# An encoder layer in f32 on one core: x is turned as it comes and kept feature-major, and the row lengths are applied in the splits

## The chip, the cores and the metric

The kernel runs on one core of one Trainium2 chip. The core has TensorE (PE, matrix products; PEld loads its weights), VectorE (DVE), ScalarE (ACT), GpSimd (POOL) and SyncE (SP), whose queue issues nearly all DMAs of this kernel; sixteen DMA engines move the data between the large memory (DRAM) and the core's own memory (SBUF). Products go to a small accumulator memory (PSUM), of which a tile of two banks holds the sums of a whole output tile. The metric is the device time in microseconds. The figure for a kernel is the median of its runs; beside it stands one profiled execution, to which all durations of the profile belong.

## The reference

One layer of a hybrid encoder is computed for a prompt of 512 rows and a sample of 64 rows, with 2048 features. What matters here is its beginning and the first residual sum:

```python
mod = jax.nn.silu(c) @ w_ada[l] + b_ada[l]
sh1, sc1, g1, sh2, sc2, g2 = jnp.split(mod[:, None, :], N_MOD, axis=-1)
h = rmsnorm(x, norm1[l]) * (1 + sc1) + sh1
mix, s_a, s_b, s_c = token_mixers(h, ...)     # h @ w_in, GLA, gated DeltaNet, @ w_out
x = x + g1 * mix
h = rmsnorm(x, norm2[l]) * (1 + sc2) + sh2    # then the FFN, the second residual sum, the final norm
```

`rmsnorm` divides each row of x by the root of its mean square (plus 1e-6). The prompt and the sample have their own modulation (`c_prompt`, `c_sample`). So x is needed twice: normed and modulated, as the input of the projections, and untouched, as the first term of the residual sum.

## The kernel before

All activations are held feature-major: 128 features on the partitions, the 576 rows (512 of the prompt, 64 of the sample) along a tile as two halves of 288, each 256 prompt rows and 32 sample rows (`HP` = 256, `HT` = 288). There are `KD` = 16 such tiles. A product in f32 precision is made of three in the faster form `fp32r`: each operand is split into a high and a low part (ACT copies the rounded high part, DVE subtracts it), and high x high, low x high and high x low are summed in PSUM (`mm6`, lines 544 and 546). Every weight tile of 512 KB passes this way: a DMA into a raw tile, `split` (lines 630 to 632) into `wh` and `wl`, products.

**The head** (`head`, from line 641) computes the modulation, brings x in, and makes the input tiles `h`. `modulation(g)` multiplies the conditioning vectors with a block of w_ada: for each of two parts (scale and shift) it goes through 16 row blocks, two at a time, in 8 steps; each step loads 512 KB into an `hraw` tile (a ring of five). Steps at rows 4 and 12 multiply the raw tile as it is in whole f32 (line 710), the others split it and multiply the parts (lines 714 and 715). The sums are turned by small products (line 720). The first call, `modulation(0)`, has 16 steps, and ahead of steps 1, 3, 5, 7 and 9 (`X_AT`) it brings in one block of x: `x_block(b)` loads 128 rows (64 for the sample) in four pieces of 512 features, sums their squares on ACT (line 673), makes the reciprocal root on DVE and POOL (lines 674, 140, 141), scales the four pieces on DVE (line 677), and turns them on PE (line 682) into PSUM, from where ACT copies them into `xT` (lines 685 and 689). Then, for g = 0 to 3, `modulation(g + 1)` is followed by the four input tiles of group g: `split_mod` makes s * xT + b on DVE (line 566), the high part on ACT (567) and the low part on DVE (568), and the tile goes at once into the narrow gates (line 829) and the first q and k projections.

**The mixers** follow, in which PE runs the projections (`in_tile`) and between them, at each tick, a step of the recurrences or of the rest of the modulation (`ada`, line 772, with tiles `xr` and `ax`).

**The residual stage** then forms w_out times the second half of the mixers' output: for each of 16 feature tiles m, 8 blocks of products (48 of them), and beside them x: `x_load(m)` reads the 128 columns of tile m from the row-major input into an `xr` tile (a ring of two, which the last modulation tiles and the loads of the mixers' output `od` also use), and `x_tile(m)` turns it by five transpositions on PE (line 147, called by `transpose4`, and line 1129) and copies it on ACT into the place of an old `h` tile (lines 1127 and 1130). `residual` adds the gated product on DVE (line 1096). The first half of the mixers' output follows in a second pass over the same tiles, then the FFN.

The order of instructions on each engine, SP's DMAs among them, is fixed when the program is built: the framework's scheduler takes them by the order in which the code emits them, as far as its own cost model has their inputs and places ready. A block under `high_priority(offset=80)` is ranked 80 instructions earlier; all weight loads and splits are. `pgt` gives PSUM tiles from a ring of two.

Of the kernel before, what the change touches and what calls it, by code (L numbers as in the profile page):

```python
# [27 lines left out]
X_AT = (1, 3, 5, 7, 9)  # L28
# [70 lines left out]
class Kern:  # L99
# [462 lines left out]
    def split_mod(self, x, s, b, hh, hl, tmp):  # L562

        nc = self.nc
        for c, q in ((slice(0, HP), 0), (slice(HP, HT), 1)):
            nc.vector.tensor_scalar(tmp[:, :, c], x[:, :, c], s[:, q:q + 1], b[:, q:q + 1], op0=ALU.mult, op1=ALU.add)
        nc.scalar.activation(hh, tmp, AF.Copy)
        nc.vector.tensor_tensor(hl, tmp, hh.bitcast(F32), op=ALU.subtract)
# [70 lines left out]
    def head(self, pool):  # L639
# [25 lines left out]
        def x_block(b):  # L665
            n = P if b < 4 else TS
            xt = [slot() for _ in range(4)]
            for q in range(4):
                f = slice(q * 512, (q + 1) * 512)
                nc.sync.dma_start(xt[q][:n], i["x_prompt"][0, b * P:(b + 1) * P, f] if b < 4 else i["x_sample"][0, :, f])  # L670
            ms4 = pool.tile([P, 8], F32, tag="ms4", bufs=2, name=self.name("ms4"))
            for q in range(4):
                A.activation(junk[:n], xt[q][:n], AF.Square, scale=float(D) ** -0.5, accum_out=ms4[:n, q:q + 1])
            V.tensor_reduce(ms4[:n, 4:5], ms4[:n, 0:4], axis=mybir.AxisListType.X, op=ALU.add)
            self.rsqrt(ms4[:, 5:6], ms4[:, 4:5], 1, n)
            for q in range(4):
                V.tensor_scalar_mul(xt[q][:n], xt[q][:n], ms4[:n, 5:6])
            per = 4 if b < 4 else 8
            for k0 in range(0, KD, per):
                ps = self.pgt()[:, 0]  # L680
                for k in range(k0, k0 + per):
                    T.transpose(ps[:, (k - k0) * n:(k - k0 + 1) * n], xt[k // 4][:n, k % 4 * P:(k % 4 + 1) * P],
                                self.c["ident"][:n, :n])
# [7 lines left out]


# [4 lines left out]
        hraw = lambda: pool.tile([P, 1024], F32, tag="hraw", bufs=5, name=self.name("hraw"))  # L697
# [415 lines left out]
    def x_load(self, m):  # L1113

        nc, i, raw = self.nc, self.i, self.xr()
        n = slice(m * P, (m + 1) * P)
        nc.sync.dma_start(raw[:, :512].rearrange("p (b t) -> p b t", b=4), i["x_prompt"][0, :, n].rearrange("(b p) n -> p b n", p=P))
        nc.sync.dma_start(raw[:TS, 512:512 + P], i["x_sample"][0, :, n])
        return raw

    def x_tile(self, m, raw):

        nc = self.nc
        t = self.slot(self.x_place(m), F32)
        nc.gpsimd.memset(t[:, :, HP:ZS], 0.0)
        ps = self.transpose4(raw[:, :512].rearrange("p (b t) -> p b t", b=4))
        nc.scalar.activation(t[:, :, :HP], ps.rearrange("p (h b) t -> p h (b t)", h=2), AF.Copy)
        ps = self.bank()
        nc.tensor.transpose(ps[:, :TS], raw[:TS, 512:512 + P], self.c["ident"][:TS, :TS])
        nc.scalar.activation(t[:, :, ZS:], self.halves(ps[:, :TS]), AF.Copy)  # L1130
        return t

# [431 lines left out]
def layer_kernel(tc, i, o):  # L1564
    nc = tc.nc
    with ExitStack() as ctx:
# [10 lines left out]
        nc.vector.memset(K.zero3, 0.0)  # L1577
        K.xd = [dp.tile([P, 2, HZ], F32, name=f"xd{m}") for m in range(KD)]
# [3 lines left out]
        with ExitStack() as early:  # L1582
            K.wp = pool(early, "wp", "right", bufs=3)
            with ExitStack() as right:
# [9 lines left out]
                with ExitStack() as st:  # L1594
# [126 lines left out]
```

## Time and profile before

| | |
|---|---|
| median of 3 runs | 2973.34 us (2972.37 to 2979.27) |
| the profiled execution | 2975.75 us, span 2974.0 us |
| mean granted clock of TensorE | 0.989 of full |
| PE busy | 2892.8 us, 97% of the span |
| DVE, ACT, POOL busy | 2106.4, 1232.6, 359.1 us |
| moved by DMA | 393.02 MB, mean 132 GB/s |

A row of the profile names the line of the kernel, the engine, the operation, and the tiles written and read (out<-in, buffer numbers left out), with a count. Busy time is the time in which an engine executes; the idle time is put down to whatever released the engine. The chain of waits goes back from the last instruction, at each step to what it waited for. The granted clock is the share of full clock that TensorE was given. Matmul ends are modelled, so the starts of successive instructions are the safer measure of PE's pace. "Whole f32" products show two records each.

### The profile page before, as it was taken

How to read it: one execution, taken by the hardware profiler on the slowest of the kernel's cores; microseconds unless marked ns; L12 is line 12 of the kernel's file. 1: busy time of each engine (PE TensorE's matmuls, PEld its weight loads, DVE VectorE, ACT ScalarE, POOL GpSimd, SP SyncE). 2: the span in 40 equal slices, each digit the busy share in tenths (PEclk: the TensorE clock that was granted, in tenths of full speed). 3: DMA queues.
4: the chain of work that ended last, by engine and by line, in shares of the span. 5: the costliest groups of instructions: out<-in, count | busy, mean ns of one | idle time of the engine just before them, and what ended most of it. 6: DMA issues, size and time to landing. Idle time of an engine off the chain costs nothing.

```text
span 2974.0 us, 52340 instructions
## 1 busy us (share of the span) xinstructions
PE 2892.8 (97%) x21128; PEld 2786.1 (94%) x21128; DVE 2106.4 (71%) x3243; ACT 1232.6 (41%) x2124; POOL 359.1 (12%) x616
## 2 busy tenths in 40 slices
PE   7998999998999999999999999999999999999998
PEld 3588999998989998999999999999999999999997
DVE  5786777775669777367888888888888865555555
ACT  6573544544244433255444444444444422222223
POOL 0015433343310001000000000000000000000000
PEclk8999999999999999999999999999999999999999
DMA  7864455544545447443333333333333463333221
GB/s 263 283 176 142 141 158 151 153 138 129 148 129 149 142 136 210 134 130 90 101 111 98 105 109 109 100 104 109 104 106 98 140 230 98 114 102 112 85 84 66
DMA packets 509446, 393.02 MB, mean 132 GB/s; under 512 B 41385, under 2 KB 438404, under 8 KB 509204
## 3 DMA queue, kind: packets, MB, share of 16 engines
q1 hardware_dynamic: 503780, 379.00, 42.8%
q0 software_dynamic: 5424, 10.68, 1.2%
q8 instruction: 167, 2.74, 0.4%
q14 instruction: 75, 0.61, 0.1%
HBM read 355.23 MB, written 34.36 MB: 131 GB/s over the span
## 4 chain that ended last, share of the span: by engine, by line
PE 86%; DVE 4%; POOL 3%; DMA 2%; issue 2%; ACT 2%; ACTq 0%; SPq 0%; POOLq 0%; DVEq 0%
PE g L544 29%; PE g L546 14%; PE g L1330 8%; PE g L1331 8%; PE g L1332 8%; PE bank L1331 3%; PE bank L1330 3%; PE bank L1332 3%; PE bank L147 1%; DVE acc L772 1%; PE bank L778 1%; POOL m L359 1%; PE bank L419 1%; POOL m L360 1%; PE bank L710 1%
## 5 line engine op out<-in xcount | busy, mean ns | idle before, releaser
L544 PE MATMUL g<-slot,wh 128*128 128x288 f32 x3168 | 551.2, 295 | 1.4 <-ACT slot L1105 0.7
L1330 PE MATMUL g<-slot,wh 128*128 128x290 f32 x1760 | 533.4, 303 | 2.6 <-ACT p L1342 2.6
L1331 PE MATMUL g<-slot,wh 128*128 128x290 f32 x1760 | 526.5, 299 | 0.0
L1332 PE MATMUL g<-slot,wl 128*128 128x290 f32 x1760 | 521.0, 296 | 0.0
L631 ACT ACTIVATE wh<-raw 128x1024 fp32r<-128x1024 f32 x223 | 236.1, 1059 | 673.4 <-PE g L544 651.9
L544 PEld LDWEIGHTS g<-slot,wh 128*128 128x128 f32 x3168 | 463.4, 188 | 2.6 <-ACT slot L1105 1.0
L544 PE MATMUL g<-hh,wh 128*128 128x288 f32 x1984 | 457.3, 310 | 1.0 <-DVE gcb L935 1.0
L544 PE MATMUL g<-hl,wh 128*128 128x288 f32 x1984 | 434.4, 299 | 0.0
L546 PE MATMUL g<-hh,wl 128*128 128x288 f32 x1984 | 430.5, 298 | 0.0
L1096 DVE SCALAR_TENSOR_TENSOR slot<-g,mod,slot 128x512 f32<-128x512 f32 (+1 forms) x448 | 201.7, 491 | 253.7 <-PE g L546 252.7
L632 DVE TENSOR_TENSOR wl<-raw,wh 128x1024 fp32r<-128x1024 f32 x223 | 272.5, 1222 | 136.5 <-ACT wh L631 134.3
L1277 ACT ACTIVATE wh<-raw 128x1024 fp32r<-128x1024 f32 x176 | 186.9, 1062 | 392.2 <-PE g L1331 388.1
L1330 PEld LDWEIGHTS g<-slot,wh 128*128 128x128 f32 x1760 | 331.2, 188 | 16.8 <-ACT p L1342 11.6
L546 PE MATMUL g<-slot,wl 128*128 128x288 f32 x1584 | 341.7, 295 | 0.0
L1332 PEld LDWEIGHTS g<-slot,wl 128*128 128x128 f32 x1760 | 336.5, 191 | 0.0
L1331 PEld LDWEIGHTS g<-slot,wh 128*128 128x128 f32 x1760 | 335.2, 190 | 0.1
L544 PEld LDWEIGHTS g<-hh,wh 128*128 128x128 f32 x1984 | 318.9, 191 | 5.1 <-DVE gcb L935 1.2
L544 PEld LDWEIGHTS g<-hl,wh 128*128 128x128 f32 x1984 | 322.4, 190 | 0.4 <-issue 0.2
L546 PEld LDWEIGHTS g<-hh,wl 128*128 128x128 f32 x1984 | 320.4, 189 | 0.3 <-issue 0.2
L546 PEld LDWEIGHTS g<-slot,wl 128*128 128x128 f32 x1584 | 255.6, 188 | 0.0
L772 DVE SCALAR_TENSOR_TENSOR acc<-xr,ct,acc 128x512 f32<-128x512 f32 x322 | 227.7, 748 | 5.6 <-DMA xr<-in_w_ada_dram 5.6
L1278 DVE TENSOR_TENSOR wl<-raw,wh 128x1024 fp32r<-128x1024 f32 x176 | 214.7, 1220 | 18.8 <-ACT wh L1277 18.7
(373 smaller groups left out, 4594.6 us busy)
## 6 DMA issues: line engine op xcount, KB each, us to landing
raw<-in_w_up_dram SPq DMA_DIRECT2D x176, 512.0 KB
raw<-in_w_in_dram SPq DMA_DIRECT2D x108, 512.0 KB
raw<-in_w_down_dram SPq DMA_DIRECT2D x88, 512.0 KB
xr<-in_w_ada_dram SPq DMA_DIRECT2D x86, 512.0 KB
hraw<-in_w_ada_dram SPq DMA_DIRECT2D x64, 512.0 KB
ax<-in_w_ada_dram SPq DMA_DIRECT2D x42, 512.0 KB
raw<-in_w_out_dram SPq DMA_DIRECT2D x32, 512.0 KB
slot<-actd SPq DMA_DIRECT2D x44, 288.0 KB
```

What stands on the lines that cost most here:

```text
L147: self.nc.tensor.transpose(ps[:, b * P:(b + 1) * P], src4[:, b], self.c["ident"])
L544: T.matmul(ps[:, h if bank is None else bank, :n], wh, x[:, h, :n], start=f, stop=False)
L546: T.matmul(ps[:, h if bank is None else bank, :n], wl, ah[:, h, :n], start=False, stop=stop)
L631: nc.scalar.activation(hi[:, :n_], raw[:, :n_], AF.Copy)
L632: nc.vector.tensor_tensor(lo[:, :n_], raw[:, :n_], hi[:, :n_].bitcast(F32), op=ALU.subtract)
L772: V.scalar_tensor_tensor(acc[s], w[:, k], col, acc[s], op0=ALU.mult, op1=ALU.add)
L1096: self.nc.vector.scalar_tensor_tensor(x1[:, :, z], ps[:, :, c], gain[:, q:q + 1], x1[:, :, z], op0=ALU.mult, op1=ALU.add)
L1277: self.nc.scalar.activation(hi, src, AF.Copy)
L1278: self.nc.vector.tensor_tensor(lo, src, hi.bitcast(F32), op=ALU.subtract)
L1330: T.matmul(ps, wh[:, j], hi, start=(c < 3 and j == 0), stop=False, skip_group_check=True)
L1331: T.matmul(ps, wh[:, j], lo, start=False, stop=False, skip_group_check=True)
L1332: T.matmul(ps, wl[:, j], hi, start=False, stop=(j == NPAIR - 1), skip_group_check=True)
```

## The change

Three things change, all in how x reaches its two uses.

- In the head, x is turned as it comes, without the norm. `x_block` becomes three parts with steps of their own: `x_load` at the old step, `x_turn` three steps later (`X_LAG`), `x_norm` four steps later. `x_norm` only computes the reciprocal root of each row's mean square, into a column of `rs`. After `modulation(0)`, `x_rows` lays these columns on diagonals and multiplies a matrix of ones with them, one product of 512 columns and one of 64, so that every partition has all row lengths along the tile (`rx`). `split_mod` then forms x * s * rx, ACT adds b while it makes the high part, and DVE forms the low part from the sum. 
- Each turned tile `xT[:, k]` is stored to DRAM (`xs[k]`, 288 KB) behind its split. In the residual stage `x_tile(m)` loads it back into the same place as before, in two DMAs (the prompt's rows in runs of 1024 bytes, the sample's in runs of 128 bytes). `x_load`, the five transpositions, the two copies on ACT and the use of `xr` are gone.
- The raw tiles of the modulation come in turn from `hraw` (five) and from the ring `raw` (three), which before served only the weights of the projections.

```diff
-X_AT = (1, 3, 5, 7, 9)
+X_AT, X_LAG = (1, 3, 5, 7, 9), 3
...
-    def split_mod(self, x, s, b, hh, hl, tmp):
-
-        nc = self.nc
+    def split_mod(self, x, r, s, b, hh, hl, tmp):
+
+        V, A = self.nc.vector, self.nc.scalar
         for c, q in ((slice(0, HP), 0), (slice(HP, HT), 1)):
-            nc.vector.tensor_scalar(tmp[:, :, c], x[:, :, c], s[:, q:q + 1], b[:, q:q + 1], op0=ALU.mult, op1=ALU.add)
-        nc.scalar.activation(hh, tmp, AF.Copy)
-        nc.vector.tensor_tensor(hl, tmp, hh.bitcast(F32), op=ALU.subtract)
+            V.scalar_tensor_tensor(tmp[:, :, c], x[:, :, c], s[:, q:q + 1], r[:, :, c], op0=ALU.mult, op1=ALU.mult)
+            A.activation(hh[:, :, c], tmp[:, :, c], AF.Identity, bias=b[:, q:q + 1])
+        for c, q in ((slice(0, HP), 0), (slice(HP, HT), 1)):
+            V.scalar_tensor_tensor(hl[:, :, c], tmp[:, :, c], b[:, q:q + 1], hh[:, :, c].bitcast(F32), op0=ALU.add, op1=ALU.subtract)
...
-        def x_block(b):
+        xt, rs = {}, pool.tile([P, 5], F32, tag="rs", bufs=1, name="rs")
+
+        def x_load(b):
...
-            for q in range(4):
-                V.tensor_scalar_mul(xt[q][:n], xt[q][:n], ms4[:n, 5:6])
...
+        def x_norm(b):
+            n = P if b < 4 else TS
+            ms4 = pool.tile([P, 8], F32, tag="ms4", bufs=2, name=self.name("ms4"))
+            for q in range(4):
+                A.activation(junk[:n], xt[b][q][:n], AF.Square, scale=float(D) ** -0.5, accum_out=ms4[:n, q:q + 1])
+            V.tensor_reduce(ms4[:n, 4:5], ms4[:n, 0:4], axis=mybir.AxisListType.X, op=ALU.add)
+            self.rsqrt(rs[:, b:b + 1], ms4[:, 4:5], 1, n)
+
+        def x_rows():
+
+            dg = slot()
+            for b in range(4):
+                V.tensor_scalar_mul(dg[:, b * P:(b + 1) * P], self.c["ident"], rs[:, b:b + 1])
+            dgs = junk[:, :TS]
+            V.tensor_scalar_mul(dgs[:TS], self.c["ident"][:TS, :TS], rs[:TS, 4:5])
+            rx = pool.tile([P, 2, HT], F32, tag="rx", bufs=1, name="rx")
+            ps = self.pgt()
+            T.matmul(ps[:, 0], self.c["ones"], dg, start=True, stop=True)
+            T.matmul(ps[:, 1, :TS], self.c["ones"][:TS], dgs[:TS], start=True, stop=True)
+            A.activation(rx[:, :, :HP], self.halves(ps[:, 0]), AF.Copy)
+            A.activation(rx[:, :, HP:], self.halves(ps[:, 1, :TS]), AF.Copy)
+            return rx
...
-        hraw = lambda: pool.tile([P, 1024], F32, tag="hraw", bufs=5, name=self.name("hraw"))
+        turns = iter("hhrhhrhr" * 99)
+
+        def hraw():
+            if next(turns) == "r":
+                return self.raw()
+            return pool.tile([P, 1024], F32, tag="hraw", bufs=5, name=self.name("hraw"))
...
-        plan = {X_AT[b]: lambda b=b: x_block(b) for b in range(5)}
-        step = iter(range(99))
-        modulation(0, lambda: plan.get(next(step), lambda: None)())
+        plan = [[] for _ in range(16)]
+        for b in range(5):
+            for f, at in ((x_load, 0), (x_turn, X_LAG), (x_norm, X_LAG + 1)):
+                plan[X_AT[b] + at].append(lambda f=f, b=b: f(b))
+        step = iter(plan)
+        modulation(0, lambda: [f() for f in next(step)])
+        rx = x_rows()
...
-                self.split_mod(xT[:, k], s1[:, k], self.mod[:, 0, k], hh, hl, tmp)
+                self.split_mod(xT[:, k], rx, s1[:, k], self.mod[:, 0, k], hh, hl, tmp)
+                nc.sync.dma_start(self.xs[k], xT[:, k])
...
-    def x_load(self, m):
-
-        nc, i, raw = self.nc, self.i, self.xr()
-        n = slice(m * P, (m + 1) * P)
-        nc.sync.dma_start(raw[:, :512].rearrange("p (b t) -> p b t", b=4), i["x_prompt"][0, :, n].rearrange("(b p) n -> p b n", p=P))
-        nc.sync.dma_start(raw[:TS, 512:512 + P], i["x_sample"][0, :, n])
-        return raw
-
-    def x_tile(self, m, raw):
+    def x_tile(self, m):
 
         nc = self.nc
         t = self.slot(self.x_place(m), F32)
+        nc.sync.dma_start(t[:, :, :HP], self.xs[m][:, :, :HP])
+        nc.sync.dma_start(t[:, :, ZS:], self.xs[m][:, :, HP:])
         nc.gpsimd.memset(t[:, :, HP:ZS], 0.0)
-        ps = self.transpose4(raw[:, :512].rearrange("p (b t) -> p b t", b=4))
-        nc.scalar.activation(t[:, :, :HP], ps.rearrange("p (h b) t -> p h (b t)", h=2), AF.Copy)
-        ps = self.bank()
-        nc.tensor.transpose(ps[:, :TS], raw[:TS, 512:512 + P], self.c["ident"][:TS, :TS])
-        nc.scalar.activation(t[:, :, ZS:], self.halves(ps[:, :TS]), AF.Copy)
         return t
...
-                    raw = K.x_load(0)
                     for m in range(KD):
                         ps = K.pgt()
                         K.gemm(ps, K.w_cols("w_out", m, 8), ob, tick=K.tick)
-                        nxt = K.x_load(m + 1) if m + 1 < KD else None
-                        K.x1.append(K.x_tile(m, raw))
-                        raw = nxt
+                        K.x1.append(K.x_tile(m))
                         K.residual(ps, K.x1[m], K.mod[:, 2, m])
```

More of the change, by code (lines that the diff above doesn't have):

```diff
@@ L681, in x_block @@
                 for k in range(k0, k0 + per):
-                    T.transpose(ps[:, (k - k0) * n:(k - k0 + 1) * n], xt[k // 4][:n, k % 4 * P:(k % 4 + 1) * P],
+                    T.transpose(ps[:, (k - k0) * n:(k - k0 + 1) * n], xt[b][k // 4][:n, k % 4 * P:(k % 4 + 1) * P],
                                 self.c["ident"][:n, :n])
@@ L1577, in layer_kernel @@
         nc.vector.memset(K.zero3, 0.0)
+        K.xs = [dp.tile([P, 2, HT], F32, name=f"xs{k}") for k in range(KD)]
         K.xd = [dp.tile([P, 2, HZ], F32, name=f"xd{m}") for m in range(KD)]
```

11 lines of the change are left out of this document (4 added, 7 removed).

## The prediction

> **What bounds the kernel now.** I read the page first, then the busy time in short stretches, then the chain of waits, PE's timeline and the queue of SP, at the two places that the change touches.
>
> ```profile
> span 2974.0 us, 52340 instructions
> PE 2892.8 (97%) x21128; PEld 2786.1 (94%) x21128; DVE 2106.4 (71%) x3243; ACT 1232.6 (41%) x2124; POOL 359.1 (12%) x616
> ```
>
> PE is busy for 97% of the span, so work that leaves PE's queue is worth its duration unless something else comes late in its place; work that leaves ACT (41%) is worth nothing by itself. The two places have different limits. The columns of the stretches are: length, then busy time and instructions of PE, PEld, DVE, ACT and POOL, the granted clock, the DMA share, GB/s.
>
> ```profile
> 15.00:20.00 5.00, 5.00 (x18) 2.31 (x17) 2.39 (x4) 2.91 (x5) 0.00 (x0) 1.00 1.06 398
> 25.00:30.00 5.00, 3.28 (x15) 2.93 (x16) 2.04 (x7) 4.11 (x12) 0.55 (x1) 0.56 1.02 377
> 40.00:45.00 5.00, 3.45 (x17) 3.46 (x18) 3.45 (x8) 2.37 (x4) 0.55 (x1) 0.50 0.59 209
> 50.00:55.00 5.00, 4.09 (x21) 2.10 (x22) 3.47 (x6) 3.43 (x7) 0.10 (x1) 0.80 0.11 11
> 100.00:120.00 20.00, 20.00 (x90) 10.89 (x88) 13.08 (x17) 9.26 (x11) 0.00 (x0) 1.00 0.85 274
> 120.00:140.00 20.00, 20.00 (x106) 13.60 (x106) 17.75 (x27) 11.92 (x14) 0.78 (x2) 1.00 0.88 292
> 1160.00:1180.00 20.00, 17.96 (x132) 17.09 (x133) 11.14 (x17) 4.89 (x9) 2.74 (x4) 1.00 1.00 260
> 1180.00:1200.00 20.00, 20.00 (x150) 19.53 (x149) 5.78 (x9) 3.42 (x7) 0.00 (x0) 1.00 0.44 124
> ```
>
> In the head, up to about 62 us, neither PE nor the DMA engines are full: PE has 3.28 and 3.45 of 5 us at half the clock, and between 50 and 55 the DMA engines move 11 GB/s where they had moved 398. From 100 to 140 PE is full. In the residual stage (about 1150 to 1266) PE is full as well, apart from the first part. What starves the head stands in the chain and in SP's waits:
>
> ```profile
> 25.08 0.17 DVE ms L674
> 26.72 3.75 PE g L682 x16
> 36.92 0.62 ACT hs L673 x2
> 41.55 1.94 PE g L682 x8
> 46.05 0.72 ACT hs L673 x2
> 50.54 1.28 DVE hs L677 x3
> 51.85 1.06 ACT wh L631
> 54.18 4.69 DMA hraw<-in_w_ada_dram
> 61.93 1.05 PE bank L720 x8
> ...
> PE g L682 <- DVE hs L677: 6.6, 3, 2.7
> SPq L630 <- PE bank L710: 38.6, 12, 9.3
> ```
>
> The row norm of an x block (squares on ACT, the sum and EPS on DVE, the power on POOL, four scalings on DVE) lies on the chain ahead of the block's transpositions: 25.08 to 26.72, 36.92 to 41.55 and 46.05 to 51.85, that is 1.6 + 4.6 + 5.8 = 12.0 us. PE itself stands 6.6 us for the scaled rows. Behind the transpositions in PE's queue wait the products L710, which read raw `hraw` tiles directly; SP waits 38.6 us for them to give back one of five tiles, and after the longest such wait the DMA of 4.69 us is on the chain.
>
> **The change part by part.** *Residual stage: five transpositions per feature tile go.* PE's timeline, one period of sixteen:
>
> ```profile
> 1178.52 0.60 PE L147 MATMUL bank<-consts,xr 128*128 128x128 f32 x4
> 1179.05 0.27 PE L1129 MATMUL bank<-consts,xr 64*128 64x64 f32 x1
> 1179.25 0.53 PE L544 MATMUL g<-hh,wh 128*128 128x288 f32 x2
> 1179.62 0.42 PE L544 MATMUL g<-hl,wh 128*128 128x288 f32 x2
> 1179.88 0.43 PE L546 MATMUL g<-hh,wl 128*128 128x288 f32 x2
> ...
> 1185.76 0.60 PE L147 MATMUL bank<-consts,xr 128*128 128x128 f32 x4
> ```
>
> From 1178.52 to 1179.25 PE turns x, 0.73 us, and the first pair of products behind it takes 0.37 where the next takes 0.26 (1179.62 to 1179.88), 0.10 more: 0.83 of the 7.24 us period. Sixteen times: **-13.3 us**. PE is full here (20.00 of 20), so this counts in full. The wait for x goes too:
>
> ```profile
> PE bank L147 <- DMA xr<-in_x_prompt_dram: 2.1, 2, 1.8
> L1127 ACT ACTIVATE slot<-bank x16: 578/582/600, 1153.5 to 1266.1; 128x512 f32<-128x512 f32 x16
> L1118 SPq DMA_DIRECT2D xr<-in_x_sample_dram x16: 482/516/935, 1145.9 to 1252.0; - x16
> od<-m POOLq DMA_DIRECT2D x16, 256.0 KB, 3.8
> od<-m POOLq DMA_DIRECT2D x16, 32.0 KB, 4.2
> ```
>
> That is **-2.1 us**, and the evictions (16 of 0.58 on ACT) go at no gain. In their place come two loads per tile from `xs`, 256 and 32 KB. On SP they replace two issues with two, about 0.5 us each, so the queue is not longer. They no longer need an `xr` tile, only the place of an old h tile, and the modulation's raw tiles have both `xr` to themselves. The load must land before the residual sum on DVE, not before a product; with two PSUM tiles PE runs ahead of that sum by one period, 7.24 - 0.83 = 6.4 us. The nearest rows for such transfers are 3.8 and 4.2 us. So I cost the loads at nothing; uncovered, each would stand for about 4.2 us less that period, nothing again, unless SP or the DMA engines are late (rival B).
>
> The 32 KB load goes in runs of 128 bytes, and the row of the same shape, 4.2 us, is slower than that of eight times its size. The Trainium skill, "DMA: Bandwidth & Descriptors", section Specifications, asks for at least 512 B for full rate; the two rows agree. By that rule the sample loads cost like the large ones, which stays below a period.
>
> *Head: the turn does not wait for the norm, and the ring is eight deep.* The 12.0 us leave the chain ahead of the transpositions, and the three more tiles cover the 4.69 us: at most -16.7. At least the 6.6 us for which PE stood should go, unless other waits move up (rival A: nothing). ACT still does twenty squares and the evictions of the transpositions, and `wh` queues behind them, so what is late next is the split of the weights. I take **-10.5**, between 6.6 and 16.7 and nearer the wait that PE shows.
>
> ```profile
> 104.61 1.88 PE L710 MATMUL bank<-hraw,cs 128*4 128x512 f32 x4
> L673 ACT ACTIVATE hs<-hs 128x512 f32<-128x512 f32 x16 | 10.1, 629 | 1.8 <-DMA hs<-in_x_prompt_dram 1.4
> L677 DVE TENSOR_SCALAR hs<-hs,ms 128x512 f32<-128x512 f32 x16 | 6.7, 482 | 2.8 <-POOL ms L141 2.8
> L566 DVE TENSOR_SCALAR tmp<-xT,s,mod 128x512 f32<-128x512 f32 x16 | 8.7, 543 | 0.1
> L566 DVE TENSOR_SCALAR tmp<-xT,s,mod 128x64 f32<-128x64 f32 x16 | 5.2, 322 | 0.0
> L568 DVE TENSOR_TENSOR hl<-tmp,hh 128x576 fp32r<-128x576 f32 x16 | 11.8, 754 | 0.3
> L1096 DVE SCALAR_TENSOR_TENSOR slot<-g,mod,slot 128x512 f32<-128x512 f32 x192 | 144.1, 750 | 237.8 <-PE g L546 237.6
> L1096 DVE SCALAR_TENSOR_TENSOR slot<-g,mod,slot 128x64 f32<-128x64 f32 x192 | 52.9, 276 | 0.0
> ```
>
> *Two products for the row lengths.* Whole f32 products over 512 columns take 1.88 / 2 = 0.94 us (the four records are two products), the one over 64 columns about the 0.27 of L1129: **+1.2 us** on PE. The five diagonals on DVE and two evictions come before the first split needs them, beside the last steps of the modulation. If that cover is gone they add at most 5 x 0.54 (the scaling of 512 columns, where a diagonal has 128) + 2 x 0.58 = 3.9.
>
> *The splits.* Two forms with two tensors of 512 and two of 64, 2 x (0.750 + 0.276) = 2.05 us on DVE per tile, for 0.543 + 0.322 + 0.754 = 1.62: 0.43 more, 6.9 in all, against 20 scalings of 0.48 (9.6) that go. DVE has 6.9 and 2.2 us free in the two stretches of 20 from 100 to 140, so the first twelve tiles (5.2 us over some 90) cost nothing; on ACT one copy to `hh` becomes two shorter ones, with 8 to 11 us of 20 free. The last four have PE behind them, at most 4 x 0.43 = 1.7: **+0.9**.
>
> *The stores of x.* Sixteen of 288 KB, 4.7 MB, issued by SP in the head, where it mostly waits for tiles. The DMA engines move 274 to 292 GB/s while PE is full and have shown 377 and 398; over the 90 us from 62 to 150 that leaves (377 - 283) x 90 = 8.5 MB. Cost nothing; without that room 4.7 MB / 283 GB/s = 16.6 us (rival C).
>
> **The sum**: -13.3 - 2.1 - 10.5 + 1.2 + 0.9 = **-23.8 us**. The profiled execution took 2975.75 us, 1.75 above its span, and 2.4 above the median of the runs, 2973.34. So 2952.0 for a profiled execution like it, and 2949.5 against the median, which is what I predict.
>
> **The rivals.** *A, the head stands still* (the ring is not eight deep in effect, because the raw tiles also serve the q and k weights, or ACT's queue holds the splits back): -13.3 - 2.1 + 1.2 + 0.9 = -13.3, 2960. For it: `wh` comes through the same ACT as the squares. Against it: the DMA engines idle at 11 GB/s for want of tiles.
>
> *B, the loads of x crowd the start of the residual stage.* Nothing but the places holds them, so SP may send many at once between 1140 and 1180, where the DMA share is already 1.00 at 260 GB/s. 4.7 MB at that rate are 18 us, and the modulation's last tiles, whose products stand in PE's queue, come late. Half of it, 9 us, would be seen: -14.8, 2958.5. Against it: the same bytes are read at that place now, and the w_out tiles are several periods ahead.
>
> *C, the stores pace the head.* If the DMA engines hold no more than the 283 GB/s seen under full PE, all 16.6 us come on top and the ring brings nothing: -15.4 + 2.1 + 16.6 = +3.3, 2976.6, slower than before. It decides from the point where the engines sustain less than 283 + 4.7 MB / 90 us = 335 GB/s; below 283 the price is full. Against it: 377 and 398 above.
>
> *D, the clock recovers with the waits.* At 25 to 30 and 40 to 45 the granted clock is 0.56 and 0.50 with PE a third idle, at 100 and after it is 1.00 with PE full. If a PE without pauses holds the clock from 25 us on, the head reaches its upper bound: -13.3 - 2.1 - 16.7 + 2.1 = -30.0, 2943. The Trainium skill, "TensorE: Matmul & The Clock Gate", section Part 1: The HAM clock gate, has the clock halved after an idle window and whole after a busy one, in line with these rows. By that rule alone D would be likelier; but the start stays bound by the arrival of weights, so PE will still pause.
>
> **How the numbers follow.** My forecast has 0.55, D 0.13, A 0.14, B 0.10, C 0.04; 0.04 are left for a new order of instructions in the long middle that loses what was won. What one measurement of this kernel can tell from no change is about 0.3%, 8.9 us, so faster means below 2964.4. The forecast and D are faster whole, A and B in three cases of four (0.18 of 0.24): 0.86. C and the rest split into 0.10 for the same and 0.04 slower. The range runs from 2938, a little below D, to 2965, past A and B with their own spread; what is left out above is C and the unnamed cases, and about 0.05 below.
>
> **What would show it.** Right: no f32 transpositions from `xr` after 1130 and a period near 6.4 us there; the L720 products of the first modulation at about 50 instead of 61.93; DMA above 300 GB/s from 40 to 55; no wait of PE for scaled rows; the end of the head about 8 us earlier. Wrong: PE waits in the residual stage that end with a load from `xs` or w_ada (B), stretches with PE below 20 and DMA near 283 GB/s in 80 to 150 (C), the clock still near 0.5 at 40 (D falls), the head's end unmoved (A).

## The result, and the profile after

The median fell by 18.2 us, from 2972.86 us (2969.48 to 2979.27, four runs) to 2954.64 us (2952.49 to 2958.58, four runs). The ratio is 0.9934, 95% interval [0.9914, 0.9954]; taken of the 2972.86 that is 19.6 us less, between 13.7 and 25.6. The profiled execution took 2952.49 us, where the prediction had 2952.0 for it and 2949.5 for the median.

The page of the changed kernel:

```profile
span 2950.7 us, 52150 instructions
PE 2872.5 (97%) x21052; PEld 2771.9 (94%) x21052; DVE 2102.8 (71%) x3244; ACT 1227.5 (42%) x2110; POOL 361.0 (12%) x616
```

The span is 23.3 us shorter (2974.0 before), and PE has 20.3 us less work (2892.8 before). Where the rest went is read from three landmarks that both kernels have: the copy of the first narrow tile out of PSUM, which ends the head, and the residual sums of tiles m = 3 and m = 15. The changed kernel's DVE, in order of time (start, duration, row):

```profile
160.85 0.76 DVE L777 COPY xr<-ps_k 128x576 f32<-128x576 f32 x1 [1.32 <-PE ps_k L546]
...
1168.24 0.94 DVE L1127 SCALAR_TENSOR_TENSOR slot<-g,mod,slot 128x512 f32<-128x512 f32 x2 [1.54 <-PE g L546]
...
1245.04 0.94 DVE L1127 SCALAR_TENSOR_TENSOR slot<-g,mod,slot 128x512 f32<-128x512 f32 x2 [4.33 <-PE g L546]
```

The same three before:

```profile
166.76 0.76 DVE L746 COPY xr<-ps_k 128x576 f32<-128x576 f32 x1 [2.35 <-PE ps_k L546]
...
1180.69 0.94 DVE L1096 SCALAR_TENSOR_TENSOR slot<-g,mod,slot 128x512 f32<-128x512 f32 x2
...
1267.41 0.94 DVE L1096 SCALAR_TENSOR_TENSOR slot<-g,mod,slot 128x512 f32<-128x512 f32 x2
```

| stretch | before | after | difference |
|---|---|---|---|
| start to the end of the head | 166.76 | 160.85 | -5.9 |
| head to residual tile 3 | 1013.93 | 1007.39 | -6.5 |
| tile 3 to tile 15 (twelve periods) | 86.72 | 76.80 | -9.9 |
| tile 15 to the end of the span | 1706.6 | 1705.7 | -0.9 |

The third row is the residual stage alone: a period went from 86.72 / 12 = 7.23 to 6.40 us, 0.83 each. The second holds the first tiles' turnings and the waits for x. So the head gave 5.9 us where the prediction had 8.4, and the rest 17.4 where it had 15.4.

**The head** in stretches (length, then busy time and instructions of PE, PEld, DVE, ACT and POOL, the granted clock, the DMA share, GB/s), the changed kernel:

```profile
20.00:40.00 20.00, 13.59 (x81) 8.81 (x79) 8.09 (x20) 17.17 (x39) 1.66 (x3) 0.99 0.96 302
40.00:60.00 20.00, 18.57 (x70) 8.55 (x71) 12.56 (x20) 13.64 (x26) 0.54 (x1) 0.84 1.01 354
```

and before:

```profile
20.00:40.00 20.00, 14.30 (x64) 8.11 (x62) 9.86 (x20) 16.87 (x39) 1.10 (x2) 0.81 0.82 285
40.00:60.00 20.00, 16.48 (x66) 9.06 (x66) 10.95 (x21) 12.03 (x22) 1.09 (x2) 0.76 0.51 167
```

From 40 to 60 the DMA engines now move 354 GB/s where they moved 167, and the clock from 20 to 40 is 0.99 where it was 0.81. What PE waits for up to 165 us, and what the chain shows there, in the changed kernel:

```profile
PE bank L606 <- DMA hs<-in_c_sample_dram: 9.9, 1, 9.9
PE bank L746 <- DVE rw L743: 5.0, 5, 1.8
PE bank L606 <- DVE cols L607: 3.4, 3, 1.8
PE g L681 <- ACT xT L684: 1.6, 5, 0.4
...
36.87 0.62 ACT hs L695 x2
37.94 0.56 POOL rs L141
38.73 1.22 DVE wl L633
40.16 0.41 PE bank L606
...
45.05 1.12 PE g L708 x2
...
50.61 0.36 PE g L709 x2
...
54.74 0.69 DVE rw L743
55.47 1.05 PE bank L746 x8
```

and before:

```profile
PE bank L605 <- DMA hs<-in_c_sample_dram: 7.2, 1, 7.2
...
PE bank L720 <- DVE rw L717: 2.4, 2, 1.4
...
PE bank L605 <- DVE cols L606: 0.2, 1, 0.2
```

The 6.6 us for the scaled rows are gone. Other waits grew: for the copy `rw` from 2.4 to 5.0 and for the copy `cols` from 0.2 to 3.4 (small copies on DVE ahead of a product), for the first conditioning vectors from 7.2 to 9.9, and for the copies of `xT` on ACT from nothing to 1.6. The chain shows what stands around the copy `cols`: the squares on ACT (36.87), the power on POOL (37.94) and a split on DVE (38.73), so the norm still delays PE, through the queues of ACT and DVE instead of through x itself. The first modulation's turning products (the eight L746, before L720) start at 55.47, 6.5 us earlier than before, and the row products (L708 and L709) now stand ahead of them.

How PE spent the time up to these turning products shows where the 6.5 us come from. The last column is a second profile of the changed kernel, called f1 below.

| up to the turning products | before | changed | f1 |
|---|---|---|---|
| their start | 61.93 | 55.47 | 57.29 |
| PE idle | 20.0 | 18.8 | 18.0 |
| PE busy | 42.0 | 36.6 | 39.3 |
| of that, row products | - | 1.5 | 2.5 |
| mean granted clock | 0.86 | 0.97 | 0.88 |

PE's idle time fell by only 1.1 us (1.9 in f1), because the other waits took back most of the 6.6. In this profile most of the gain up to here is products that took less time, at a higher granted clock.

### The profile page after: what moved, and what is told of

The parts are those of the page before. It is cut to its first block, busy times and chain, and to the rows that moved or that the text cites. A ratio compares the mean times of both kernels' runs of the same rounds, so it can differ in the third digit from the quotient of the medians.

```text
span 2950.7 us, 52150 instructions
## 1 busy us (share of the span) xinstructions
PE 2872.5 (97%) x21052; PEld 2771.9 (94%) x21052; DVE 2102.8 (71%) x3244; ACT 1227.5 (42%) x2110; POOL 361.0 (12%) x616
## 4 chain that ended last, share of the span: by engine, by line
PE 86%; POOL 4%; DVE 4%; DMA 3%; ACT 2%; issue 2%; SPq 0%; ACTq 0%; POOLq 0%; DVEq 0%
PE g L544 29%; PE g L546 14%; PE g L1349 8%; PE g L1350 8%; PE g L1351 8%; PE bank L1350 3%; PE bank L1349 3%; PE bank L1351 3%; POOL m L359 1%; POOL m L360 1%; PE bank L147 1%; PE bank L809 1%; PE bank L419 1%; DVE acc L803 1%; PE bank L736 1%
## 5 line engine op out<-in xcount | busy, mean ns | idle before, releaser
L632 ACT ACTIVATE wh<-raw 128x1024 fp32r<-128x1024 f32 x239 | 253.0, 1058 | 678.2 <-PE g L544 652.2
L633 DVE TENSOR_TENSOR wl<-raw,wh 128x1024 fp32r<-128x1024 f32 x239 | 291.9, 1222 | 93.1 <-ACT wh L632 90.0
L1296 ACT ACTIVATE wh<-raw 128x1024 fp32r<-128x1024 f32 x176 | 186.8, 1061 | 391.2 <-PE g L1350 384.0
L1349 PEld LDWEIGHTS g<-slot,wh 128*128 128x128 f32 x1760 | 331.3, 188 | 18.1 <-ACT p L1361 11.8
L1297 DVE TENSOR_TENSOR wl<-raw,wh 128x1024 fp32r<-128x1024 f32 x176 | 214.7, 1220 | 18.6 <-ACT wh L1296 18.4
```

Of the source, the lines that this page charges most:

```text
L632: nc.scalar.activation(hi[:, :n_], raw[:, :n_], AF.Copy)
L633: nc.vector.tensor_tensor(lo[:, :n_], raw[:, :n_], hi[:, :n_].bitcast(F32), op=ALU.subtract)
L1296: self.nc.scalar.activation(hi, src, AF.Copy)
L1297: self.nc.vector.tensor_tensor(lo, src, hi.bitcast(F32), op=ALU.subtract)
L1349: T.matmul(ps, wh[:, j], hi, start=(c < 3 and j == 0), stop=False, skip_group_check=True)
```

## The experiments

All kernels at a glance. The head's end is the start of the copy shown above; the mixers are the stretch from there to residual tile 3. Those two come from the one profiled execution of each kernel, the median from all its runs, and the ratio is to runs of the kernel before taken beside it. Those had medians from 2971.92 to 2975.99, so kernels are better compared by the ratio.

| kernel | head's end | mixers | median | ratio, 95% |
|---|---|---|---|---|
| before | 166.76 | 1013.9 | 2972.86 | |
| changed | 160.85 | 1007.4 | 2954.64 | 0.9934 [0.9914, 0.9954] |
| e1 head only | 159.90 | 1013.5 | 2971.05 | 0.999 [0.9981, 0.9998] |
| e2 residual only | 169.28 | 1010.1 | 2963.29 | 0.9964 [0.9951, 0.9977] |
| e3 ring of five | 170.76 | 1008.4 | 2958.21 | 0.9945 [0.9932, 0.9958] |
| e4 ring of eight only | 165.36 | 1013.7 | 2972.13 | 0.9999 [0.999, 1.0008] |
| f1 changed, again | 160.41 | 1013.2 | 2954.04 | 0.9937 [0.9923, 0.9951] |
| f2 vectors first | 161.45 | 1008.9 | 2950.48 | 0.9929 [0.991, 0.9947] |
| f3 stores twice | 172.21 | 1004.9 | 2961.79 | 0.9965 [0.9953, 0.9978] |
| f4 one load | 163.80 | 1003.6 | 2953.75 | 0.9938 [0.9924, 0.9953] |
| g1 lag of one | 160.65 | 1004.5 | 2952.23 | 0.9918 [0.9903, 0.9933] |
| g2 ring of six | 168.70 | 1009.8 | 2961.92 | 0.9949 [0.9934, 0.9963] |
| g3 vectors first, one load | 162.25 | 1006.3 | 2955.72 | 0.9932 [0.9917, 0.9946] |
| h1 ring of five, again | 169.84 | 1013.5 | 2960.31 | 0.9947 [0.9933, 0.9961] |

Two kernels were profiled twice. The head's end came back within 0.4 us (changed and f1) and 0.9 us (e3 and h1), the mixers only within 5.8 and 5.1 us. So one profile tells the head to about 1 us, and the whole time to no better than some 5.

### The two halves apart

*The head alone*: the changed kernel without the store, and with the old way of bringing x into the residual stage.

```diff
-                nc.sync.dma_start(self.xs[k], xT[:, k])
...
+        ps = self.transpose4(raw[:, :512].rearrange("p (b t) -> p b t", b=4))
+        nc.scalar.activation(t[:, :, :HP], ps.rearrange("p (h b) t -> p h (b t)", h=2), AF.Copy)
```

> The new head with the old residual stage (x read row-major again and turned there by five transpositions per tile; nothing is stored). Theory: the two parts add, and the head is worth what its end moved in the changed kernel, 166.76 to 160.85 us: about 6 us less than before (ratio near 0.998), a period of 7.2 us in the residual stage, and a wait of PE for x there of about 2 us. Rival 1 (the stores hold the head back in the changed kernel): without them the head ends clearly before 160, and the gain is 9 us or more. Rival 2 (the head's gain is eaten again in the mixers, so that all the gain is in the residual stage): no difference, 0 to 2 us.

Its head ends at 159.90, 6.9 us before the old one. In its residual stage x is turned again, and this is PE's timeline and wait there:

```profile
1200.17 0.60 PE L147 MATMUL bank<-consts,xr 128*128 128x128 f32 x4
...
1207.40 0.60 PE L147 MATMUL bank<-consts,xr 128*128 128x128 f32 x4
...
PE bank L147 <- DMA xr<-in_x_prompt_dram: 2.0, 2, 1.8
```

The period is 7.23 us and the wait for x 2.0, both as before. The ratio, 0.999, is worth 3.0 us, between 0.6 and 5.6: less than the 6 us that the theory took from the head's end, more than nothing.

*The residual stage alone*: the kernel before, which stores its `xT` and loads it back. Left out: its stored x is the normed one, so the residual sum gets x divided by the row length; the work is otherwise that of the changed stage.

```diff
+                nc.sync.dma_start(self.xs[k], xT[:, k])
...
+        nc.sync.dma_start(t[:, :, :HP], self.xs[m][:, :, :HP])
+        nc.sync.dma_start(t[:, :, ZS:], self.xs[m][:, :, HP:])
```

> The old head (x scaled by its norm, then turned; ring of five), whose turned tiles are stored and loaded back in the residual stage. What is left out: the residual sum gets x divided by its row length instead of x; shapes and work are those of the changed kernel. Theory: sixteen times 0.83 us of transpositions and 2 us of waits, with up to 3 us at the change to the second pass: 15 to 18 us less than before, a period of 6.4 us. Rival (stores pace the head): the head ends more than 3 us later than 166.76 and the gain is 12 us or less.

The twelve periods take 76.81 us (1179.40 to 1256.21), the same 6.40 each. But the old head, with sixteen stores in it, ends 2.5 us later than without them (169.28). The ratio, 0.9964, is worth 6.8 to 14.6 us. That is 10.7 us, where 15 to 18 were expected; the later head accounts for 2.5 of the difference. So the residual stage is the larger part of the gain.

The two parts do not add up to the whole: 3.0 and 10.7 are 13.7, where the changed kernel gains 19.6 (18.7 in f1, where 18 to 23 were expected). The stores explain some 2 us, because they cost e2's old head 2.5 and the new head less than 1 (see below). The rest is not explained.

### The two edits of the head apart

*The turn without the norm, with the old ring of five*:

```diff
-        turns = iter("hhrhhrhr" * 99)
...
+        hraw = lambda: pool.tile([P, 1024], F32, tag="hraw", bufs=5, name=self.name("hraw"))
```

> The changed kernel with the raw tiles of the modulation in the old ring of five. Theory (norm off the way to the turn and the ring share the head's gain): first modulation ends between 56 and 61 us, the whole is 2 to 5 us slower than the changed kernel. Rival 1 (the ring does all): the head ends at 166 or later, 6 us or more slower. Rival 2 (the ring brings nothing in the head, PE's first work at 9.9 us instead of 7.2 even costs): the same or up to 2 us faster than the changed kernel, PE's first product earlier.

*The ring of eight, in the kernel before*:

```diff
-        hraw = lambda: pool.tile([P, 1024], F32, tag="hraw", bufs=5, name=self.name("hraw"))
+        turns = iter("hhrhhrhr" * 99)
+        def hraw(): ...
```

> The kernel before with the modulation's raw tiles in a ring of eight, x scaled before it is turned. Theory: the ring alone cannot help where the transpositions stand in front of the products that free the tiles: 0 to 3 us less than before, PE still waits about 6 us for scaled rows. Rival (the ring does all): 5 us or more less than before, first modulation ended near 55.

By the head's end each edit alone brings next to nothing. The turn alone ends at 170.76, 1.5 us behind e2's 169.28, which has the same stores (its turning products come at 62.93, where 56 to 61 was expected); the ring alone at 165.36, 1.4 us ahead of before. Both together end at 160.85. The head with five tiles, in stretches, and what SP and PE wait for in its head:

```profile
40.00:45.00 5.00, 4.09 (x10) 1.99 (x10) 1.12 (x6) 1.95 (x6) 0.55 (x1) 0.50 0.77 287
45.00:50.00 5.00, 5.00 (x21) 2.50 (x21) 1.58 (x4) 2.73 (x7) 0.54 (x1) 0.50 0.00 1
...
SPq L631 <- PE bank L731: 34.2, 10, 4.1
...
PE bank L736 <- DVE wl L633: 8.0, 13, 1.1
```

With five tiles the DMA engines still come to rest, at 1 GB/s from 45 to 50: SP stands 34.2 us for tiles that PE's raw products hold. With eight tiles and the old turn it is the other way round:

```profile
PE g L682 <- DVE hs L677: 6.2, 3, 3.9
```

PE still stands 6.2 us for scaled rows (6.6 before), while with five tiles and the new turn it stands 8.0 us for late splits. So by the waits each edit alone leaves the starvation that the other one removes. The clock has a part in it: up to their turning products e3's PE is idle for 19.0 us, no longer than the changed kernel's 18.8, and busy for 43.9 instead of 36.6, at a mean clock of 0.84 instead of 0.97.

*Six tiles* show whether the last tiles matter:

```diff
-        turns = iter("hhrhhrhr" * 99)
+        turns = iter("hhhhhr" * 99)
```

> The changed kernel with one raw tile of the projections' ring in six turns, five and one, instead of three in eight. Theory (the ring must hold the tiles that PE reads raw while the turns stand in front of them, so each tile counts): between the ring of five (head ended at 170.8) and that of eight (160.4 to 160.9), near 166 to 168. Rival (a threshold: one more tile is enough): near 161.

168.70, a little later than the 166 to 168 that were expected: a sixth tile gives about 1.6 of the 9.7 us that lie between five (e3 and h1, mean 170.3) and eight (changed and f1, mean 160.6).

The runs of e3 did not fit its head: by the ratios it is only 3 us behind the changed kernel, and 5.7 us ahead of e2, whose head ends 1.5 us earlier. So the ring of five was run once more:

> The changed kernel with the modulation's raw tiles in the ring of five alone, once more and with more rounds. In its first execution that was profiled the head ended at 170.76 us, 10 us later than with eight tiles (160.4 and 160.85), but the median of its runs was 2958.21, only some 2 us behind. If the ring of eight is worth what that profile shows, the ratio to the kernel before is 0.9955 or more (-13.3 us: the residual stage's -17.4 and +4.0 at the head), and the head of this profile ends at 168 us or later. If the first profile caught a disturbed head and turning x without the norm does most of the work by itself, the ratio is 0.9945 or less, the head of this profile ends between 160 and 166 us, and the low granted clock between 40 and 55 us (0.50) is gone from it.

```profile
40.00:45.00 5.00, 3.23 (x9) 1.82 (x10) 1.40 (x8) 3.18 (x9) 0.55 (x1) 0.50 0.65 239
45.00:50.00 5.00, 4.75 (x26) 1.99 (x24) 1.00 (x4) 2.73 (x7) 0.54 (x1) 0.94 0.00 0
...
169.84 0.76 DVE L772 COPY xr<-ps_k 128x576 f32<-128x576 f32 x1 [1.44 <-PE ps_k L546]
```

Each theory was half right. The late head is real: 169.84, with the same rest of the DMA engines (0 GB/s from 45 to 50) and a clock of 0.50, here until 45. The ratio is as good as the first time, 0.9947, so the whole time does not show what that head shows. Over all kernels with the new turn, the new residual stage and one set of stores, the three with five or six tiles (e3, h1, g2) have a mean ratio of 0.9947 and the six with eight (changed, f1, f2, f4, g1, g3) 0.9931: 4.7 us, where the heads' ends lie 8.2 us apart (means 169.8 and 161.6). The ring is worth something, and some of what it gains at the head's end is not seen in the runs. The mixers do not show it given back: they take 1008.2 us in the mean of these kernels and f3 and e2, and the old 1013.9 less the turnings and waits of 5.4 would be 1008.5. With a spread from 1003.6 to 1013.5 this can't be settled by single profiles, and it stays open.

### The stores

*Every tile stored twice*, the second time to a place that nothing reads:

```diff
                 nc.sync.dma_start(self.xs[k], xT[:, k])
+                nc.sync.dma_start(self.xs2[k], xT[:, k])
```

> The changed kernel that stores every turned tile twice, 9.4 MB instead of 4.7. Theory (the DMA engines have room): the head ends 0 to 3 us later, the whole within 3 us of the changed kernel. Rival (the stores pace the head at 283 GB/s): 16 us more.

> The changed kernel once more, beside the others of this call. Theory: 18 to 23 us less than before; the parts measured alone (head 3.1, residual stage 10.7 us by their medians) add to less than that because each part alone keeps a loss that the other takes away. Rival (the parts just add and the first figure was a lucky chip): 12 to 15 us less.

The first 4.7 MB cost the new head 0.5 to 0.95 us (159.90 without them, 160.41 and 160.85 with them), which is no more than one profile can tell. The second 4.7 MB cost 172.21 - 160.41 = 11.8 us, and the medians differ by 7.7; 0 to 3 us were expected, and 16 by the rival. Two stretches and a wait of the kernel that stores twice:

```profile
100.00:105.00 5.00, 2.06 (x9) 0.77 (x7) 3.39 (x4) 3.17 (x3) 0.00 (x0) 1.00 1.05 388
125.00:130.00 5.00, 3.40 (x20) 2.35 (x18) 4.40 (x7) 2.39 (x4) 0.32 (x1) 1.00 1.05 396
...
PE bank L736 <- DMA raw<-in_w_ada_dram: 4.2, 2, 2.2
```

PE has 2.06 and 3.40 of 5 us while the DMA engines run at 388 and 396 GB/s, and PE now waits for weights to arrive. 4.72 MB in 11.8 us would be 400 GB/s, about the highest rate seen, as if each further byte cost PE its whole transfer. That is an estimate: in between, the engines of this kernel also rest (110 GB/s from 110 to 115, 19 from 145 to 150), and the second stores stand in SP's queue as well, which no run separates. The changed kernel has 399 GB/s in one stretch itself:

```profile
120.00:125.00 5.00, 5.00 (x26) 2.84 (x24) 4.75 (x8) 3.13 (x6) 0.32 (x1) 1.00 1.05 399
```

but with PE at 5.00 of 5. One set of stores just fits. The Trainium skill, "DMA: Bandwidth & Descriptors", section Specifications, gives a limit of about 358 GB/s for one core at the large memory; further down the page takes that as the share of a core whose neighbour streams too. These stretches, of a kernel on one core, lie above it, and the measurement decides.

### The start, the lag and the loads

In the changed kernel SP issues four weight loads ahead of the constants and the vectors where before it issued two. SP's queue, changed:

```profile
0.74 2.00 SPq L631 DMA_DIRECT2D hraw<-in_w_ada_dram  x4
2.78 0.68 SPq L112 DMA_DIRECT2D consts<-in_consts_dram  x1
```

The first product then starts at 11.48 instead of 9.56. *The constants and vectors first*:

```diff
+        with self.tc.high_priority(offset=4 * AHEAD):
+            for _ in range(3):
+                next(vectors)
...
+        with tc.high_priority(offset=4 * AHEAD):
+            K.load_consts(K.cp, LONG)
```

> The changed kernel with the loads of the constants, the conditioning vectors, biases and norms ranked ahead of the first weight loads. Theory (the deeper ring lets four weight loads go ahead of them, so that PE's first product starts at 11.48 us instead of 9.56): the first product near 9.5, the head ends 1 to 2 us earlier than 160.85, the whole 1 to 2 us less than the changed kernel. Rival (the weights' arrival sets the head's pace anyway): first product earlier, first modulation still at 55.5, the whole unchanged.

```profile
8.45 0.67 PE L741 MATMUL bank<-wh,cst 128*66 128x512 f32 x1 [3.00 <-ACT wh L632]
```

The first product starts 3 us earlier and the head ends at 161.45, no earlier. Up to the turning products, which start at 56.76, PE is idle for 16.2 us, less than in the changed kernel and in f1 (18.8 and 18.0), but busy for 40.5, longer than in both (36.6 and 39.3). So the early start does not reach the head's end. That the arrival of the weights takes it back, which the rival expected, is not shown: from 62 to 165 the changed kernel's PE waits only 0.3 us for split weights. The ratio, 0.9929, can't be told from the changed kernel's.

*The turn one step behind the load, not three*:

```diff
-X_AT, X_LAG = (1, 3, 5, 7, 9), 3
+X_AT, X_LAG = (1, 3, 5, 7, 9), 1
```

> The changed kernel with x turned one step behind its load instead of three (the norm two behind). Theory (what the head paces is the arrival of the weights and of x, not the place of the turn in the order of the code): first modulation ended at 55 to 58, head ended at 159 to 162, the whole within 2 us of the changed kernel. Rival (the lag of three keeps PE from standing for x): PE waits for x or its copies and the head ends 3 us or more later.

The head ends at 160.65, where the changed kernel's ends. The lag itself is not what removed the wait for x; leaving out the norm is.

*x brought back in one load per tile*, with the sample's rows padded in `xT` so that the whole tile is stored and loaded as it lies:

```diff
-        nc.sync.dma_start(t[:, :, :HP], self.xs[m][:, :, :HP])
-        nc.sync.dma_start(t[:, :, ZS:], self.xs[m][:, :, HP:])
+        nc.sync.dma_start(t, self.xs[m])
```

> The changed kernel with the turned tiles laid out as the residual tiles are (the gap of two columns included), stored and loaded whole: one load of 290 KB in runs of 2320 bytes per tile instead of two with runs of 1024 and 128 bytes. Theory (the loads land a period ahead of their use): the DMA share between 1140 and 1180 falls below 0.95, PE gains nothing, the whole within 1 us of the changed kernel. Rival (the short runs crowd the DMA engines and hold w_ada back): 2 us or more less, the last modulation's products earlier against the first residual tile.

At the start of the residual stage, the changed kernel:

```profile
1140.00:1160.00 20.00, 19.19 (x146) 18.99 (x145) 16.26 (x25) 6.71 (x10) 8.46 (x21) 1.00 0.98 292
1160.00:1180.00 20.00, 20.00 (x155) 20.00 (x154) 7.91 (x12) 4.34 (x5) 0.00 (x0) 1.00 1.06 290
...
L1148 SPq DMA_DIRECT2D slot<-xs x16: 524/580/956, 1134.1 to 1171.4; - x16
L1149 SPq DMA_DIRECT2D slot<-xs x16: 525/610/975, 1134.8 to 1172.1; - x16
```

and with one load per tile:

```profile
1140.00:1160.00 20.00, 19.58 (x148) 19.38 (x148) 16.20 (x26) 6.83 (x9) 7.25 (x10) 1.00 1.02 324
1160.00:1180.00 20.00, 20.00 (x155) 20.00 (x154) 8.89 (x13) 4.85 (x7) 0.00 (x0) 1.00 1.11 322
```

All thirty-two loads of x are sent within 38 us, 1134.1 to 1172.1, and the DMA engines are full there in both kernels, at 290 to 292 GB/s with the short runs (279 to 306 in f1) and 322 to 324 without. The expected fall of the DMA share below 0.95 did not come. PE is as busy in the one as in the other, and the twelve periods take 76.81 us here and 76.80 there, so nothing is gained in this stage; the ratio is the same (0.9938). The head of this profile ends 3 us later and its mixers are 4 to 10 us shorter, which the edit does not explain. That short runs cost the engines rate is in line with the Trainium skill, "DMA: Bandwidth & Descriptors", section Specifications, which asks for 512 B a run.

Both together bring nothing more than each:

> The changed kernel with the vectors' loads first and with one load per residual tile, the two edits that cost nothing alone. Theory: each is hidden, and so is their sum: within 3 us of the changed kernel, 15 to 21 us less than before. Rival (the early start of PE and the shorter queue on SP add up): 23 us less than before, or more.

The head ends at 162.25 and the ratio is 0.9932. No kernel tried is clearly faster than the changed one.

## Why the prediction was right, and where it was off

The sum was -23.8 us against a profiled execution, and the span came out 23.3 us shorter. That it is so close is partly luck: two terms were off by 2 us and more in opposite directions, and the pair of profiles flatters the change. The profile before lay 2.9 us above its median and the one after 2.1 us below its own; the medians are 18.2 us apart, so by the runs the sum was 4 to 6 us too large. That is where the 5.1 us between the median and the predicted 2949.5 come from.

- *Five transpositions per tile, -13.3 us: right.* The period is 6.40 us against 7.23, 0.83 as worked out; twelve periods gave 9.9 us in the changed kernel, and 9.9 in e2, which keeps the old head but for the stores. It held because PE is at 20.00 of 20 there.
- *The wait for x, -2.1 us: right.* e1, which keeps the old loads, keeps 2.0 us of it; the changed kernel has no such wait.
- *Loads of x at nothing: right*, though they crowd as rival B said (38 us, DMA share 0.98 to 1.06). The crowd did not reach PE: f4 lets the engines run a tenth faster there and its periods stay the same.
- *Residual terms together, -17.4 instead of -15.4.* The 2.0 more lie between head and tile 3 and after tile 15, in stretches that differ by up to 10 us between executions, so they are not put down to the change. By the runs the stage is worth less, 10.7 in e2 (6.8 to 14.6), or 13.2 with the 2.5 us that its old head lost to the stores.
- *The head's transpositions and ring, -10.5: the term that was mis-sized.* The first modulation's turning products came at 55.47 (57.29 in f1) instead of 61.93, which is 6.5 and 4.6 us, and not "about 50". With the row products counted in full the term comes to some 8.0 and 7.1, an estimate. The step that failed is the one that took a value above the 6.6 us of PE's wait because the load of 4.69 us would be covered as well. The wait went, but up to this mark PE's idle time fell by only 1.1 and 1.9 us: the copy `cols` took 3.2 us more, the late first vectors 2.7 (the first product starts 1.92 us later), the copies of `xT` 1.6. Much of what was gained came from PE's busy time instead, and for that the sum had no term. The prediction named the split of the weights as late next; it was these copies, with the norm and a split ahead of `cols` on the chain. That by the head's end the two edits work only together (e3 and e4) was in none of its steps. By the runs the head alone (e1) is worth 3.0 us, where its three terms add up to 8.4.
- *Row-length products, +1.2, and splits, +0.9: near enough, as far as can be told.* The row products took 1.5 us, and 2.5 in f1, where the larger one ran at half clock. The splits lie behind the turning products; from there to the head's end it is 105.38 us after and 103.12 in f1, 104.83 before: +0.5 and -1.7 for the 0.9 predicted.
- *Stores at nothing: right in the result, wrong in the working.* They cost the new head 0.5 to 0.95 us, and the old one 2.5 (e2). The room was put at 8.5 MB, from 377 GB/s held over 90 us; f3 stores 9.4 MB and ends 12.3 us behind the head without stores (172.21 - 159.90). At the 400 GB/s of the second set that is 4.9 MB too much, so the room was about 4.5 MB, an estimate from these rows.
- *Rival A, a head that stands still: no by its end, nearly so by the runs.* The end of the head moved by 5.9 and 6.4 us in the two profiled executions, but e1's runs by 0.6 to 5.6. Its reason was half right: DVE's and ACT's queues hold work back.
- *Rival C, stores that pace the head: its mechanism exists, one set of stores later.* It would have decided with 335 GB/s or less; the engines hold up to 399.
- *Rival D, a clock that recovers: in part.* From 20 to 40 the clock is 0.99 instead of 0.81 (0.88 in f1), and summed over slices of 10 us the head up to 170 us loses 5.1 us of full clock (6.8 in f1) where it lost 10.3. But it did not hold from 25 on: from 40 to 45 it is 0.68, and 0.50 in f1, the sign by which the prediction would drop D. Nor is it all: f2 loses 8.5 up to its head's end and ends it at 161.45, 5.3 us earlier than before. Among the kernels with eight tiles and one set of stores, the heads that lost 5.1 to 6.8 end between 160.41 and 160.85 (changed, f1, g1) and those that lost 8.5 between 161.45 and 163.80 (f2, f4, g3), so some of the head's end may hang on the clock. The clock gate of the Trainium skill, "TensorE: Matmul & The Clock Gate", section Part 1: The HAM clock gate, would make D the likelier case. The trace agrees only in part: the clock falls where PE pauses in the head, but with five tiles it is 0.50 from 45 to 50 too, where PE has 5.00 of 5 and its last pause ended at 41.3.
- *What would show it*: the period, the vanished wait for scaled rows and the DMA rate of 40 to 55 came as said (374 GB/s from 40 to 45, 322 from 50 to 55; in f1 384 and 225, with 346 between):

```profile
40.00:45.00 5.00, 4.39 (x21) 2.63 (x21) 1.72 (x4) 3.05 (x8) 0.00 (x0) 0.68 1.04 374
50.00:55.00 5.00, 4.70 (x16) 1.48 (x14) 4.43 (x7) 3.42 (x6) 0.00 (x0) 1.00 0.96 322
```

The turning products "at about 50" and the head "about 8 us earlier" did not.

## What to carry to other kernels

Work that leaves a queue which is busy in every slice of a stage was worth its duration to a tenth of a microsecond here; a wait that leaves a stage with several waits is worth what the next wait in line leaves of it, so look for the small copies that share an in-order queue with the work you move. Where a ring of tiles and a late producer starve the same engine, try them together: by the head's end each alone gave next to nothing here, though by the runs the turn alone gave some 5 us (e3 and h1 beside e2). Split PE's time into idle and busy before putting a gain down to a wait, since a changed clock moves the busy part. And size the room for extra transfers by doubling them: the first set cost next to nothing in the new head, the second nearly its whole length.

## What was not expected of the hardware

Transfers have a sharp knee in the new head: the first 4.7 MB of stores cost up to 0.95 us, the second 11.8 by the head's end. In the old head the first cost 2.5.

The clock also dips where PE has no idle time at all. In the changed kernel's mixers, the products ahead of a dip and the stretch with it:

```profile
1101.87 1.90 PE L809 MATMUL bank<-consts,acc 128*128 128x1 f32 x16
...
1105.00:1110.00 5.00, 5.00 (x29) 5.00 (x28) 2.84 (x6) 1.05 (x3) 0.00 (x0) 0.69 0.12 14
```

Read in slices of 1 us, the clock falls at about 1104.7, some 1 us after a run of sixteen products of one column. After 300 us, each of the two profiles of this kernel has two dips without a pause of PE ahead of them, and each begins within about 1 us of the end of such a run, the first or the third of three. The kernels before and e1 have the same two, g1 and f2 neither, so the run does not always lead to a dip. That these narrow products are the cause is suggested, not shown.

The other dips come with or right after a pause of PE. Again not every pause has one. The changed kernel, whose PE has just waited 2.64 us, at full clock:

```profile
876.85 1.08 PE L419 MATMUL bank<-qc,m 128*128 128x64 f32 x8 [2.64 <-DVE m L1676]
...
880.00:890.00 10.00, 10.00 (x82) 10.00 (x82) 9.14 (x23) 4.19 (x7) 0.00 (x0) 1.00 0.02 5
```

and f1, the same kernel behind the same wait:

```profile
878.39 1.94 PE L419 MATMUL bank<-qc,m 128*128 128x64 f32 x8 [2.64 <-DVE m L1676]
...
880.00:890.00 10.00, 10.00 (x62) 10.00 (x62) 7.29 (x20) 3.76 (x7) 0.00 (x0) 0.75 0.11 32
```

From 880 to 890 one execution had the full clock and 82 products, the other 0.75 and 62, with PE at 10.00 of 10 in both. Read in slices of 1 us up to 1900 us, every dip of these two profiles loses 1.7 us of full clock or two, three or four times that, as if half the clock were taken for some 3.4 us at a time. After 300 us the dips add up to 11.9 us of full clock in the one and 18.7 in the other, 6.8 us, while their mixers differ by 5.8. That the dips make the spread between executions is what these two suggest; why the same wait costs a dip in one and not in the other was not found.
